# Fourier layer: sequence tables scaled by one root per tile, odd sums as extra columns of the eight-row products, even outputs added by DMA

## The chip, the cores and the metric

One core of a Trainium2 chip runs the whole program. Its engines are PE (matrix products into eight PSUM banks of 128 x 512 f32), DVE and ACT (elementwise work, both can read PSUM), POOL (elementwise work without PSUM, and issuer of the DMA transfers that add to or convert what they write) and SP (issuer of plain DMA transfers). Each engine works its own instructions in order and waits on semaphores for the others. All DMA queues share 16 DMA engines. The metric is the device time of one execution in microseconds (us), the median of several.

## What is computed

Two sequences of 512 tokens and 1024 features each go through two layers. The change lies in the token mixer of the first:

```python
def fourier_mix(h, w_out):
    hg = h.astype(jnp.float32).reshape(B, S, N_FGROUPS, F_GROUP)      # 8 groups of 128 features
    f = jnp.fft.fft2(hg, axes=(1, 3), norm="ortho").real
    return f.reshape(B, S, D_MODEL).astype(h.dtype) @ w_out

x = x + fourier_mix(rms_norm(x, fourier_norm[0]), fourier_w_out[0])
x = x + sq_relu_mlp(rms_norm(x, mlp_norm[0]), mlp_w_up[0], mlp_w_down[0])
x = x + gqa_attention(rms_norm(x, attn_norm[0]), ...)
x = x + sq_relu_mlp(rms_norm(x, mlp_norm[1]), mlp_w_up[1], mlp_w_down[1])
return rms_norm(x, final_norm)
```

## The kernel before

The two sequences q = 0 and q = 1 pass the Fourier layer one after the other, in about the first 90 us; behind that comes the first MLP. All engines' orders in this layer are written out by hand: the code emits instructions in the order in which each engine shall work them.

**Front.** For each sequence the 512 tokens lie in four tiles xa[q, t] of 128 tokens by 1024 features, sorted so that tokens s and S-s meet. Features are sorted so that feature d and its mirror stand in the two halves of 512. `Front(q, c)` handles tiles 2c and 2c+1: `squares` (ACT, sum of squares per token), `gain` (DVE, times the norm's gain), `plus` and `minus` (DVE, sum and difference of the two halves; `plus_there` has a DMA transfer on POOL's queue add one half to the other in place), `chain` (the six small steps of the inverse root), `scale_both` (q = 0, c = 0: ACT multiplies sum, difference and an eight-column extract by the root), and `combine` (DVE, folds the two tiles of c = 1, or of q = 1, into one sum and one difference).

**Sequence transform.** For q = 0 the products are plain f32 (`exact_even`, `exact_odd`): the sums or differences of three folded tiles k against cosine and sine tables, for four blocks j of 128 features, two PSUM banks each. `exact_nyq` does the same for the eight-column extracts, one of the features 64 of each group. For q = 1 the products are split into float32r high and low parts (`seq_part`, `seq_nyq`, `mm3` of three products). ACT and DVE move each block out of PSUM (`seq_evac`).

**Feature transform.** `feat_stage` multiplies each block by the feature tables (even part u, odd part v), adds the eight-row piece (`feat_nyq`) and picks the odd sums (`pickX`, L553) into 72 rows, which `nyq_out` copies into un[q].

**Output products.** `Fold(j)` loads the output weights' two halves, takes the difference on DVE (`minus`) and has a DMA transfer on POOL's queue add the other half in place (L646); high and low parts follow on ACT and DVE. `FoldNyq` prepares 72 rows of weights (wn.w) for un[q], by a trip through HBM (L677, L679). `odd_outs` gives eight odd results, `even_outs` eight even ones, each one PSUM bank. For q = 0 ACT writes the odd results with both signs into xs[0, i] (`odd_put`), DVE adds the even ones to both halves (`even_put`, L726), and then a DMA transfer on POOL's queue adds the input x (`add_input`, L730). For q = 1 the input is loaded into xs[1, i] first (`load_xs`, L168, on SP's queue behind a store of xs[0, 2], L212), and DVE adds even and odd results from PSUM (`even_add`, L708 and L709).

**The norm of the MLP.** During the second transform ACT squares xs[0, i] (`square`, L178), eight times, each time behind an evacuation, and POOL adds the squares (L182). After the third even output of q = 1, PE sums them over partitions (`blocks.root`, L191), DVE and ACT take the root (L141 to L146), and after the fourth PE spreads it by transposes (L199).

Fillers (`idle`, L576) are products whose result nobody reads; 12 run before and 39 after the transposes of the gain (L359).

Of the kernel before, what the change touches and what calls it, by code (L numbers as in the profile page):

```python
# [44 lines left out]
def trunk_kernel(ctx, tc, x_in, xt_in, y_out, tables, rope, gfour, gcol, grow, gfin,  # L45
# [271 lines left out]
    def load_x(q, t, queue=nc.sync):  # L317
        xa[q, t] = slot([P, D], F32)
        queue.dma_start(xa[q, t], x_in[q][t * P : (t + 1) * P, :])
# [22 lines left out]
    def begin():  # L342
# [5 lines left out]
        for t in range(2, 4):  # L348
            load_x(0, t)
        exact_table(5)  # L350
        exact_table(6)
# [39 lines left out]
    def eights(x):  # L391
        return x[:, 0:512:64].unsqueeze(1).broadcast_to([P, 5, 8])

    class Front:


        def __init__(self, q, c):
            self.q, self.c = q, c
            self.ss, self.r = small(2), small(2)
            self.steps = rsqrt_steps(self.r[:, :2], self.ss[:, :2], 2, 1.0 / D)  # L400
            self.xg, self.p, self.m = [None] * 2, [None] * 2, [None] * 2

        def squares(self, i):
            sumsq(xa[self.q, 2 * self.c + i], self.ss[:, i : i + 1])

# [19 lines left out]
        def chain(self, a, b):  # L425
            for step in self.steps[a:b]:
                step()
            if b == 6 and self.c == 0 and self.q:
                self.rm = small(1)
                nc.gpsimd.tensor_mul(self.rm[:, :1], self.r[:, 1:2], mask)  # L430
# [5 lines left out]
        def scale_both(self, i):  # L436
            if i == 0:
                self.n = sm.tile([P, 2, 5, 8], F32, tag="ny", name=nm("ny"), bufs=2, padded_shape=[P, 2, 8, 8])
            for out, x in ((self.p[i], self.p[i]), (self.n[:, i], eights(self.m[i])), (self.m[i], self.m[i])):
                nc.scalar.activation(out, x, AF.Copy, scale=self.r[:, i : i + 1])  # L440
            parts.append((self.p[i], self.m[i], self.n[:, i]))

        def combine(self):
            (p1, p2), (m1, m2), r, w = self.p, self.m, self.r, 8
            stt = nc.vector.scalar_tensor_tensor
            if self.q == 0:
                n = sm.tile([P, 5, 8], F32, tag="ny", name=nm("ny"), bufs=2, padded_shape=[P, 16, 8])
                stt(n, eights(m2), r[:, 1:2], eights(m1), ALU.mult, ALU.add)
# [4 lines left out]
            n = sm.tile([P, 2, 64], F32R, tag="ny", name=nm("ny"), bufs=2)  # L453
            nc.gpsimd.memset(f32(n), 0.0)
# [13 lines left out]
            ny[self.q, self.c] = n  # L468

# [39 lines left out]
    def exact_nyq(k, o):  # L509
        nc.tensor.matmul(o[0:40, :258], parts[k][2].rearrange("p a b -> p (a b)"), cosX[k], start=k == 0, stop=k == 2)  # L510
# [26 lines left out]
    def feat_nyq(u, j, first):  # L537
        nyt = nyqs[0][:, j * P : (j + 1) * P]
        nc.tensor.matmul(u[:, :258], nyt, an, start=first, stop=not first)
        return u  # L540

    def feat_stage(q, j, a, b, an, en, u=None):
        if q == 0:
            nc.tensor.matmul(u[:, :258], ftX[:, :P], a, start=False, stop=True)
        else:
            u = ps()
            mm3(u[:, :258], ft(0)[:, 0:P], ft(1)[:, 0:P], a[:, 0], a[:, 1], True, False)
            feat_nyq(u, j, False)
        v = ps()
        pick = slice(6 - 2 * j, 78 - 2 * j)  # L550
        if q == 0:
            nc.tensor.matmul(v[:, :256], ftX[:, P:], b, start=True, stop=True)
            nc.tensor.matmul(en[0:72, :258], pickX[:, pick], a, start=j == 0, stop=j == 3)  # L553
        else:
            mm3(v[:, :256], ft(0)[:, P:], ft(1)[:, P:], b[:, 0], b[:, 1], True, True)
            ent = tabs[2][:, 516:594][:, pick]
            nc.tensor.matmul(en[0:72, :258], ent, a[:, 0], start=j == 0, stop=False)
            nc.tensor.matmul(en[0:72, :258], ent, a[:, 1], start=False, stop=j == 3)
# [4 lines left out]

    def nyq_out(q, en):
        t = slot([P, 258], F32R)[0:72]
        nc.scalar.copy(t, en[0:72, :258])
        nc.vector.tensor_sub(t[64:72], en[64:72, :258], f32(t[64:72]))
# [3 lines left out]
    nc.gpsimd.memset(f32(an), 0.0)  # L571

    def idle(o, n):

        for _ in range(n):
            nc.tensor.matmul(o[:, :256], filler, filler.unsqueeze(1).broadcast_to([P, 2, P]), start=True, stop=True)  # L576

    def transform(q, mid=lambda: None, hook=lambda at, j: None):
        on, ov = ps(), [(ps(), ps()) for _ in range(3)]
        if q == 0:  # L580
            for k in range(2):
                for j in range(3):
                    exact_even(k, j, ov[j][0])
                exact_nyq(k, on)
                for j in range(3):
                    exact_odd(k, j, ov[j][1])
            mid()
            exact_nyq(2, on)
        else:
            seq_nyq(q, 0, on)  # L590
            for j in range(3):
                seq_part(q, j, 0, *ov[j])
            mid()
            seq_nyq(q, 1, on)
        en = ps()
        nc.scalar.copy(an[0:40], on[0:40, :258])
        nc.vector.tensor_sub(an[32:40], on[32:40, :258], f32(an[32:40]))
        ab = []
        for j in range(3):
            if q == 0:  # L600
                exact_odd(2, j, ov[j][1])
                exact_even(2, j, ov[j][0])
            else:
                seq_part(q, j, 1, *ov[j])
            ab.append(seq_evac(q, *ov[j]))
            hook("seq", j)
        us = [None] * 4
        if q == 0:
            us[0] = feat_nyq(ps(), 0, True)
        feat_stage(q, 0, *ab[0], an, en, us[0])  # L610
        hook("feat", 0)
        o3 = ps(), ps()
        if q == 0:
            for k in range(3):
                exact_even(k, 3, o3[0])
            for k in range(3):
                exact_odd(k, 3, o3[1])
        else:
            for c in range(2):
                seq_part(q, 3, c, *o3)  # L620
        ab.append(seq_evac(q, *o3))
        hook("seq", 3)
        if q == 0:
            us[1:] = [feat_nyq(ps(), j, True) for j in range(1, 4)]
        feat_stage(q, 1, *ab[1], an, en, us[1])
        hook("feat", 1)
        feat_stage(q, 2, *ab[2], an, en, us[2])
        hook("feat", 2)
        feat_stage(q, 3, *ab[3], an, en, us[3])
        nyq_out(q, en)  # L630
        hook("feat", 3)

# [3 lines left out]
    class Fold:  # L636
# [7 lines left out]
        def minus(self):  # L644
            nc.vector.tensor_sub(self.b, self.a, self.b)
            nc.gpsimd.dma_start(self.a, w_four[1, self.j], accum_op=ALU.add)  # L646

        def odd(self):
            hi, lo = lent()
            split(hi, lo, self.b)  # L650
            wo.append((hi, lo))
# [5 lines left out]
        def even_lo(self):  # L657
            w = self.w
            nc.vector.tensor_sub(w[1], self.a, f32(w[0]))
            we[self.j] = w  # L660

    class FoldNyq:
# [7 lines left out]
        def load(self):  # L670
# [7 lines left out]
            for r, i in ((0, 0), (32, 1), (64, 0)):  # L678
# [43 lines left out]

    def even_put(q, fo, o):
# [9 lines left out]
    with tc.manual_schedule(engines={ET.PE, ET.Activation, ET.DVE, ET.Pool, ET.SP}):  # L733
        gr, halves_gr = begin()
        gc = cons.tile([P, 4 * KC], F32, name="gc")
        cosX = [exact[0][:, :258], exact[0][:, 514:772], exact[1][:, 256:514]]
# [1384 lines left out]
```

## Time and profile before

| | |
|---|---|
| median of 3 runs | 1672.95 us (1672.71 to 1673.36) |
| the profiled execution | 1673.12 us, its span 1671.3 us |
| granted PE clock, mean | 0.999 |
| PE busy | 1661.9 us, 99% |
| DVE, ACT, POOL busy | 76%, 52%, 24% |

The page of the profile gives busy shares of the engines over the span, and the chain of work that ended last: from the last instruction back to what released it, and so on. Other views answer for a window of time: each engine's instructions in order of time ("start, duration, engine, line, operation, written <- read, shapes, what ended the idle time before it"), who waited for whom, and the busy time of each engine, the granted clock and the DMA engines' share in given windows. Lines such as L726 are lines of the kernel before. A busy PE is a PE with products in flight; products are pipelined, so the distance between starts says more than the duration of one.

### The profile page before, as it was taken

What the parts mean: (1) busy time and instruction counts of PE and PEld (TensorE: products, weight loads), DVE (VectorE), ACT (ScalarE), POOL (GpSimd) and SP (SyncE); (2) the same over time, 40 slices, a digit from 0 to 9 for tenths busy, and PEclk for the clock granted to TensorE, in tenths of its full rate; (3) what the DMA queues carried; (4) which work ended last, traced back from release to release, by engine and by line L of the source; (5) the groups of instructions that cost most, each with busy time, mean ns of one, the idle gap of its engine ahead of it and who ended that gap; (6) DMA issues with size and microseconds to landing.
All of it is one profiled execution on the core that took longest, in us unless ns stands there. A gap on an engine that the chain in (4) does not pass through costs nothing.

```text
span 1671.3 us, 22288 instructions
## 1 busy us (share of the span) xinstructions
PE 1661.9 (99%) x7843; PEld 1387.8 (83%) x7843; DVE 1267.0 (76%) x1851; ACT 872.1 (52%) x1540; POOL 394.3 (24%) x364
## 2 busy tenths in 40 slices
PE   9999999999999999999999999999999999999998
PEld 8988887888888888888888888888888888888887
DVE  8879776557886869869888877777855487878875
ACT  7766444446342435447688855554454552433334
POOL 3321444221000001325444303004422220000002
PEclk9999999999999999999999999999999999999999
DMA  9843554449775757425501156334544696757532
GB/s 306 257 158 118 204 195 172 151 170 373 250 228 165 248 170 236 168 77 200 166 1 39 64 176 223 117 120 167 211 145 166 221 375 194 233 158 236 178 104 101
DMA packets 122192, 302.48 MB, mean 181 GB/s; under 512 B 12344, under 2 KB 13496, under 8 KB 122080
## 3 DMA queue, kind: packets, MB, share of 16 engines
q1 hardware_dynamic: 98720, 253.53, 43.9%
q0 software_dynamic: 8960, 21.05, 6.0%
q10 hardware_dynamic: 14400, 26.48, 4.2%
q8 instruction: 61, 1.00, 0.2%
q14 instruction: 51, 0.42, 0.1%
HBM read 217.59 MB, written 82.38 MB: 179 GB/s over the span
## 4 chain that ended last, share of the span: by engine, by line
PE 97%; DVE 1%; DMA 0%; ACT 0%; issue 0%; POOL 0%; DVEq 0%; POOLq 0%; ACTq 0%
PE ps L940 74%; PE ps L83 6%; PE ps L81 6%; PE ps L82 6%; PE ps L1535 2%; PE ps L576 0%; PE ps L1514 0%; DMA raw<-w_up 0%; PE ps L191 0%; PE ps L507 0%; PE ps L504 0%; DVE w L87 0%; DVE raw L990 0%; PE ps L199 0%; DVE raw L989 0%
## 5 line engine op out<-in xcount | busy, mean ns | idle before, releaser
L940 PE MATMUL ps<-u,w 128*128 128x512 f32 x4944 | 1130.9, 389 | 1.2 <-DVE t L1018 1.2
L940 PEld LDWEIGHTS ps<-u,w 128*128 128x128 f32 x4944 | 926.6, 188 | 195.9 <-ACT u L973 1.7
L86 ACT CAST w<-raw 128x1024 fp32r<-128x1024 f32 (+1 forms) x216 | 213.7, 994 | 311.5 <-PE ps L940 234.3
L87 DVE TENSOR_TENSOR w<-raw,w 128x1024 fp32r<-128x1024 f32 (+1 forms) x216 | 252.0, 1170 | 75.7 <-ACT w L86 75.4
L86 ACT CAST u<-u 128x1024 fp32r<-128x1024 f32 x144 | 145.0, 1047 | 85.1 <-PE ps L940 36.4
L87 DVE TENSOR_TENSOR u<-u,u 128x1024 fp32r<-128x1024 f32 x144 | 174.3, 1239 | 17.3 <-ACT u L86 16.0
L940 PE MATMUL ps<-u,u 128*128 128x512 f32 x600 | 143.3, 389 | 0.0
L1150 DVE TENSOR_TENSOR u<-ps,u 128x512 f32<-128x512 f32 x160 | 109.9, 688 | 39.8 <-PE ps L940 37.3
L1177 POOL DMA_DIRECT2D raw<-w_sum x32 | 27.7, 865 | 468.2 <-DMA raw<-w_sum 170.8
L1058 POOL TENSOR_TENSOR u<-u 128x512 f32<-128x512 f32 x28 | 37.0, 1321 | 425.9 <-ACT u L955 425.9
L940 PEld LDWEIGHTS ps<-u,u 128*128 128x128 f32 x600 | 112.5, 188 | 24.1 <-ACT u L973 0.4
L81 PE MATMUL ps<-u,u 128*128 128x512 f32 (+2 forms) x340 | 128.7, 380 | 0.0
L83 PE MATMUL ps<-u,u 128*128 128x512 f32 (+2 forms) x340 | 123.7, 365 | 0.0
L82 PE MATMUL ps<-u,u 128*128 128x512 f32 (+2 forms) x340 | 123.6, 365 | 0.0
L182 POOL TENSOR_TENSOR t<-t,t 128x512 f32<-128x512 f32 (+1 forms) x54 | 79.2, 1470 | 187.0 <-ACT t L178 186.1
L954 ACT ACTIVATE t<-t 128x512 f32<-128x512 f32 x64 | 40.5, 632 | 109.2 <-DVE t L1027 95.7
L83 PEld LDWEIGHTS ps<-u,u 128*128 128x128 f32 x340 | 64.2, 189 | 10.5 <-DVE u L87 0.3
L87 DVE TENSOR_TENSOR u<-ps,u 128x512 fp32r<-128x512 f32 (+3 forms) x112 | 68.2, 636 | 5.6 <-ACT u L86 5.0
L82 PEld LDWEIGHTS ps<-u,u 128*128 128x128 f32 x340 | 64.4, 189 | 8.5 <-DVE u L87 0.3
L81 PEld LDWEIGHTS ps<-u,u 128*128 128x128 f32 x340 | 64.4, 189 | 7.8
L1014 DVE TENSOR_TENSOR t<-ps,u 128x512 f32<-128x512 f32 x32 | 22.0, 689 | 59.5 <-PE ps L940 55.8
L86 ACT CAST u<-ps 128x512 fp32r<-128x512 f32 (+3 forms) x112 | 59.5, 557 | 7.7 <-PE ps L1535 6.1
(270 smaller groups left out, 2024.6 us busy)
## 6 DMA issues: line engine op xcount, KB each, us to landing
raw<-w_up SPq DMA_DIRECT2D x80, 512.0 KB, 4.6
u<-spill_t SPq DMA_DIRECT2D x60, 512.0 KB, 6.7
raw<-w_sum SPq DMA_DIRECT2D x56, 512.0 KB, 5.5
u<-spill_b SPq DMA_DIRECT2D x45, 512.0 KB, 6.3
spill_t<-u SPq DMA_DIRECT2D x84, 256.0 KB, 2.0
spill_b<-t ACTq DMA_DIRECT2D x60, 256.0 KB, 4.4
raw<-w_row SPq DMA_DIRECT2D x28, 512.0 KB, 5.0
park<-u SPq DMA_DIRECT2D x24, 512.0 KB, 4.6
```

The lines of the kernel that those rows point to most:

```text
L81: nc.tensor.matmul(out, lh, rh, start=first, stop=False)
L82: nc.tensor.matmul(out, lh, rl, start=False, stop=False)
L83: nc.tensor.matmul(out, ll, rh, start=False, stop=last)
L86: hi = nc.scalar.copy(dst_hi, src)
L87: return hi, eng.tensor_sub(dst_lo, src, f32(dst_hi))
L182: nc.gpsimd.tensor_add(acc[q][:, :n], acc[q][:, :n], s[:, :n])
L940: nc.tensor.matmul(o, w[x][:, sl], h[k][y], start=first and k + i == 0, stop=k == n - 1 and i == 2, skip_group_check=not first)
L954: nc.scalar.activation(t, src, AF.Relu)
L1058: eng.tensor_sub(t[:, 0], b12, b11)
L1150: return nc.vector.tensor_add(x, o, x)
L1177: nc.gpsimd.dma_start(s[:, 1], w[:, 3], accum_op=ALU.add)
L1535: nc.tensor.transpose(pt[:, t * P : (t + 1) * P], probs[t][:, sc * P : (sc + 1) * P], ident)
```

## The change

1. For the first two tiles of q = 0, each has its own root (`root`), and the root is multiplied into the 514 table columns that meet this tile (`table`) and no longer into sum, difference and extract. Tables are laid out anew, so that each tile has its own. The table loads and the tile loads alternate on SP's queue, and the feature table is loaded behind the first weights.
2. The odd sums of the features, which were picked by four products of 72 rows, come as DVE reductions of the sums (`odd_sums`), which ACT writes as 24 more columns per half into the extract (`put_sums`); `exact_nyq` then gives 56 rows, and `put_low` makes un[0] from them. The four products with `pickX` go. The weights' 72 rows move to other places (8, 16, 40).
3. All four blocks of q = 0 run through the sequence transform together in eight PSUM banks (`transform_exact`), and the eight-row products come behind them. The fillers become 23, and 9 more that multiply a zero weight and add to an open bank stand before the third tile.
4. Even results of q = 0 are copied by ACT (`even_put`), and two DMA transfers per pair on POOL's queue add them to xs[0, i] behind the input (`add_even`).
5. Orders change: all four weight differences come together, weights are split later, the gains and sums of q = 1 come earlier on DVE, two of the four tiles of q = 1 are loaded only when the second odd weight is split, the tables of q = 1 are loaded later, and small pieces of work change engines.

```diff
-        for t in range(2, 4):
-            load_x(0, t)
+        load_x(0, 2)
         exact_table(5)
-        exact_table(6)
+        load_x(0, 3)
...
+    def odd_sums(k):
+        s = small(8)
+        x = parts[k][0].rearrange("p (g d i) -> p g d i", g=8, i=2)[:, :, :, 1]
+        nc.vector.tensor_reduce(s, x, AX.X, ALU.add)
+        return s
+
+    def put_sums(k, s):
+        nc.scalar.copy(parts[k][2][:, :, 1:], s.unsqueeze(1).unsqueeze(1).broadcast_to([P, 2, 3, 8]))
...
-    def scale_both(self, i):
+    def table(self, i):
+        t = exact[i][:, :514]
+        nc.scalar.activation(t, t, AF.Copy, scale=self.r[:, i : i + 1])
...
-        nc.tensor.matmul(o[0:40, :258], parts[k][2].rearrange("p a b -> p (a b)"), cosX[k], ...)
+        nc.tensor.matmul(o[0:56, :258], parts[k][2].rearrange("p a b c -> p (a b c)")[:, :56], cosX[k], ...)
...
-            nc.tensor.matmul(en[0:72, :258], pickX[:, pick], a, start=j == 0, stop=j == 3)
...
+    def put_low(on):
+        norm = 1.0 / math.sqrt(S * P)
+        low = un[0]
+        nc.scalar.activation(low[0:56], on[0:56, :258], AF.Copy, scale=norm)
+        nc.vector.scalar_tensor_tensor(low[32:56], on[32:56, :258], norm, f32(low[32:56]), ALU.mult, ALU.subtract)
...
+    def transform_exact(mid, hook):
+        ov = [(ps(), ps()) for _ in range(4)]
+        for k in range(2):
+            for j in range(4):
+                exact_even(k, j, ov[j][0])
+            for j in range(4):
+                exact_odd(k, j, ov[j][1])
+        idle(ov[3][1], 9, an[:, :P])
+        mid()
+        ab = []
+        for j in range(4):
+            exact_odd(2, j, ov[j][1])
+            exact_even(2, j, ov[j][0])
+            ab.append(seq_evac(0, *ov[j]))
+            hook("seq", j)
+        on = ps()
+        for k in range(3):
+            exact_nyq(k, on)
+        put_an(on)
+        put_low(on)
...
     def even_put(q, fo, o):
-        x = xt(q, fo)
-        both = x.rearrange("p (h n) -> p h n", h=2)
-        nc.vector.tensor_add(both[:, :, 1:], o[:, 1:256].unsqueeze(1).broadcast_to([P, 2, 255]), both[:, :, 1:])
-        nc.scalar.copy(x[:, 0:257:256], o[:, 0:257:256])
+        if fo % 2 == 0:
+            even_part[fo // 2] = slot([P, 2, 512], F32)
+        nc.scalar.copy(even_part[fo // 2][:, fo % 2, :257], o[:, :257])
+
+    def add_even(q, i):
+        x, e = xs[q, i], even_part[i]
+        nc.gpsimd.dma_start(x[:, :, :257], e[:, :, :257], accum_op=ALU.add)
+        nc.gpsimd.dma_start(x[:, :, 257:], e[:, :, 1:256], accum_op=ALU.add)
...
-        idle(ps(), 39)
+        idle(ps(), 23)
...
+                fold[1].odd_hi()
+                low = fold[1].odd_lo()
+                for t in range(2, NT):
+                    behind(load_x(1, t), low, sync=True)
...
-        for fo in range(4, 6):
-            odd_put(0, fo, o[fo])
-        g0.combine()
         for k in range(4):
             table(k)
...
-        even(5)
-        g1.scale(slice(1, 2))
-        even(6)
         g1.combine()
         g1.split_hi()
+        even(5)
+        add_even(0, 2)
+        g1.split_lo()
+        even(6)
         even(7)
-        g1.split_lo()
+        add_even(0, 3)
```

POOL's queue, before, from the tables of the second sequence to the first addition of squares. u_579 and u_612 are sums of tiles of q = 1 (`plus_there`), u_441 to u_444 are xs[0, 0] to xs[0, 3] with their input:

```order
L329 DMA u_594<-dcos 128x774
L329 DMA u_596<-dsin 128x1024
L329 DMA u_598<-dalt 128x594
L329 DMA u_600<-dfeat 128x512
L419 DMA u_579<-u_579 128x512
L419 DMA u_612<-u_612 128x512
L730 DMA u_441<-xt 128x1024
L730 DMA u_442<-xt 128x1024
L730 DMA u_443<-xt 128x1024
L454 MEMSET ny_748 128x128
L730 DMA u_444<-xt 128x1024
L182 TENSOR_TENSOR t_846<-t_846,t_862 128x512
```

The same stretch now, from the end of the first tile's odd outputs to the last tile sum (L438 is `plus_there`, L784 `add_input`; u_441, u_443, u_445 and u_447 are now xs[0, 0] to xs[0, 3]):

```order
L438 DMA u_554<-u_554 128x512
L784 DMA u_441<-xt 128x1024
L438 DMA u_582<-u_582 128x512
L784 DMA u_443<-xt 128x1024
L438 DMA u_596<-u_596 128x512
L329 DMA u_601<-dcos 128x774
L329 DMA u_603<-dsin 128x1024
L329 DMA u_605<-dalt 128x594
L329 DMA u_607<-dfeat 128x512
L438 DMA u_616<-u_616 128x512
L784 DMA u_445<-xt 128x1024
L784 DMA u_447<-xt 128x1024
```

And right behind it, the additions of the even outputs (L780 and L781, `add_even`) up to the first addition of squares:

```order
L780 DMA u_441<-u_639 128x2x257
L781 DMA u_441<-u_639 128x2x255
L780 DMA u_443<-u_670 128x2x257
L781 DMA u_443<-u_670 128x2x255
L780 DMA u_445<-u_728 128x2x257
L781 DMA u_445<-u_728 128x2x255
L780 DMA u_447<-u_773 128x2x257
L781 DMA u_447<-u_773 128x2x255
L182 TENSOR_TENSOR t_859<-t_859,t_875 128x512
```

The first two input additions moved ahead of the tables, the tables moved behind three tile sums, and eight transfers now stand between the last input addition and the additions of squares.

ACT's order in the second transform, before: a square of xs[0, 0] stands between two evacuations (L86), and waits for one transfer of POOL's queue (DMASW is such a transfer's semaphore).

```order
L86 CAST u_840<-ps_797 128x258 [waits PE_49]
L86 CAST t_841<-ps_798 128x256 [waits PE_49]
L178 ACTIVATE t_846<-u_441 128x512 [waits DMASW0_49]
L86 CAST u_856<-ps_799 128x258 [waits PE_49]
L86 CAST t_857<-ps_800 128x256 [waits PE_49]
```

Now:

```order
L86 CAST u_853<-ps_810 128x258 [waits PE_49]
L86 CAST t_854<-ps_811 128x256 [waits PE_49]
L178 ACTIVATE t_859<-u_441 128x512 [waits DMASW4_49,DMASW5_49,DMASW1_49,Pool_49]
L86 CAST u_869<-ps_812 128x258 [waits PE_49]
L86 CAST t_870<-ps_813 128x256 [waits PE_49]
```

No row moved; the square now waits for three transfers, the input's and the two of the even outputs.

SP's store of xs[0, 2] and what stands behind it, before and then now:

```order
L212 DMA park<-u_443 128x1024 [waits DMAHW6_49,DMASW2_49,Activation_49]
L168 DMA u_780<-xt 128x1024 [waits DMAHW7_49,DMAHW1_49]
L168 DMA u_782<-xt 128x1024 [waits DMAHW2_49,DMAHW0_49]
L168 DMA u_784<-xt 128x1024 [waits DMASW7_49]
L168 DMA u_786<-xt 128x1024 [waits DMASW1_49]
```

```order
L212 DMA park<-u_445 128x1024 [waits DMASW1_49,DMASW2_49,DMASW0_49,DMAHW6_49,Activation_49,Pool_49]
L168 DMA u_793<-xt 128x1024 [waits DMAHW7_49,DVE_49]
L168 DMA u_795<-xt 128x1024 [waits DMAHW5_49,DMAHW0_49,Activation_49]
L168 DMA u_797<-xt 128x1024 [waits DMAHW1_49,PE_49]
L168 DMA u_799<-xt 128x1024 [waits DMAHW2_49,PE_49]
```

The order is the same; the store's wait now takes in the transfers that add the even outputs to xs[0, 2].

More of the change, by code (lines that the diff above doesn't have):

```diff
@@ L751, in trunk_kernel @@
+        f0.gain(0, 1, halves_gr[1])
+        nc.scalar.copy(gr[:, 512:], halves_gr[1])
+        f0.root(0, 2, 6)
+        f0.table(0)
+        f0.plus(0)
+        f0.minus(0)
+        f0.squares(1)
+        wn.load()
+        fold = [Fold(0)]
+        exact_table(6)
+        fold += [Fold(j) for j in range(1, 4)]
+        for t in range(2):
+            load_x(1, t)
+        nc.sync.dma_start(gc, gcol)
+        f0.gain(1)
+        f0.root(1, 0, 3)
         f1.squares(0)
-        f0.scale_both(0)
@@ L753, in trunk_kernel @@
[L753 removed]
+        f0.plus(1)
+        f0.root(1, 3, 4)
         f0.minus(1)
[L755 to L756 removed]
+        f0.root(1, 4, 6)
+        f0.table(1)
         f1.squares(1)
         f1.chain(1, 2)
[L759 removed]
+        f0.low(0)
+        f0.low(1)
+        ftX = exact[2][:, :256]
+        f1.gain(0)
         f1.minus(0)
         f1.gain(1)
[L762 removed]
+        sums3 = []
         def mid():
             f1.chain(0, 1)
+            f1.chain(2, 3)
```

330 lines of the change are left out of this document (167 added, 163 removed).

## The prediction

> **What bounds the kernel now.** I read the busy shares and the chain that ended last first, then the waits of PE in the first 230 us (the change ends before 100 us; behind that each engine runs the same instructions in the same order as before).
>
> ```profile
> PE 1661.9 (99%) x7843; PEld 1387.8 (83%) x7843; DVE 1267.0 (76%) x1851; ACT 872.1 (52%) x1540; POOL 394.3 (24%) x364
> ...
> PE 97%; DVE 1%; DMA 0%; ACT 0%; issue 0%; POOL 0%; DVEq 0%; POOLq 0%; ACTq 0%
> ```
>
> ```profile
> PE ps L576 <- DVE mask L369: 1.2, 1, 1.2
> PE ps L199 <- DVE s L146: 0.2, 1, 0.2
> ```
>
> PE is the chain: it stands still for 1.4 us in 230, and once it has started it runs without a hole until the root of the second sequence. So a change in the Fourier layer can gain only PE work that it takes away, and loses whatever hole it makes. The second thing to read is the DMA engines, by stage (columns behind the engines: granted PE clock, DMA share, GB/s):
>
> ```profile
> 41.00:53.40 12.40, 12.40 (x105) 12.40 (x105) 11.87 (x25) 9.51 (x30) 3.87 (x5) 1.00 0.64 163
> 53.40:65.30 11.90, 11.90 (x102) 11.88 (x101) 9.24 (x23) 9.84 (x28) 6.93 (x7) 1.00 1.01 215
> 65.30:72.60 7.30, 7.30 (x63) 7.30 (x62) 4.03 (x13) 6.48 (x15) 4.08 (x4) 1.00 0.98 367
> ```
>
> From 53.4 us on they are full, at 215 GB/s while POOL's adding transfers run and at 367 while plain loads run. Only between 45 and 51 us are they empty, as half-microsecond windows show (window, its length, clock, DMA share, GB/s):
>
> ```profile
> 42.00:42.50 0.50, 1.00 1.22 441
> 45.50:46.00 0.50, 1.00 0.00 0
> ...
> 46.50:47.00 0.50, 1.00 0.49 86
> 47.00:47.50 0.50, 1.00 1.04 184
> 47.50:48.00 0.50, 1.00 1.09 193
> 48.00:48.50 0.50, 1.00 0.39 62
> 48.50:49.00 0.50, 1.00 0.00 0
> ...
> 50.00:50.50 0.50, 1.00 0.00 0
> 57.00:57.50 0.50, 1.00 0.98 197
> ```
>
> The four windows from 46.5 us are one transfer alone: a 256 KB piece added in place within the on-chip memory (L419). It occupies all 16 engines for half of 0.49+1.04+1.09+0.39, 1.5 us, or 1.4 us at its steady 188 GB/s; I use 1.4. A 512 KB addition of the input at the 197 GB/s of the last row takes 2.6 us. Such a transfer thus costs twice what a plain load of its size does (441 GB/s above).
>
> **What the change takes from PE.** The chain of waits gives the prices:
>
> ```profile
> 1.17 2.93 PE ps L576 x12
> 5.81 5.40 PE ps L576 x39
> 12.52 0.56 PE ps L510 x2
> 22.28 0.43 PE ps L553 x2
> 30.77 0.12 PE ps L82
> 70.21 0.79 PE ps L191 x8
> 72.66 0.44 PE ps L199 x4
> ```
>
> Sixteen of the 39 fillers go: 16 x 5.40/39 = 2.2 us. The four picking products go (L553, each a pair of records, 0.43): 1.7 us. Nine fillers at 0.12 to 0.14 come in: 1.2 us. The products of eight-row sums grow from 40 rows to 56, which changes no column count, so I leave 0.56 each. Sum: 2.7 us less work, the most that this change can gain, and 0.16% of the time. Part of it goes to waiting. The third pair of products needs the combined tile:
>
> ```profile
> 17.20 0.75 DVE L449 SCALAR_TENSOR_TENSOR t<-t,s,t 128x512 f32<-128x512 f32 x1
> ```
>
> DVE reaches that row through the same gains, sums and differences as before, with one more chain of five small operations (0.16 us each), and without a hole before or now; so the tile is ready at about 17.8 to 18 us again, while PE with fillers is there at 17.3. I take 0.5 us for this, and the first product of the odd outputs comes 2.2 us earlier than now. Scaling a table (ACT, 514 columns) instead of two sums (512 each) is one ACT operation less per tile, and the tables are scaled before PE arrives; no cost. The three new reductions (128x8 from 256 each) have no row; between the smallest and the largest DVE operation they cost 0.2 to 1.2 us, and I take 0.4 by their element count. They stand behind the combination, where the eight products of the third pair (eight times 0.43, 3.5 us) hide them; without this cover up to 1.2 us would show.
>
> Taking the even outputs off DVE frees eight additions (5.2 us with the copies) at a place where DVE is full, but PE did not wait for DVE there, so it is worth nothing on PE's path.
>
> **What the change adds to the DMA engines.** Each pair of even outputs is now copied by ACT and added by two transfers on POOL's queue, 257 and 255 columns of two rows: eight transfers of 262 KB, the size and kind of the L419 piece. At 1.4 us they are 11.2 us of full DMA. Their rows are 1 KB where L419's are 2 KB, which no row here prices. Bounds: 0.65 us each if they moved at the plain 441 GB/s, 2.8 if a 1 KB row cost as much as a 2 KB one; I take 1.4, the nearest row.
>
> [...]
>
> What stands around them:
>
> ```profile
> 34.54 0.86 POOL L419 DMA_DIRECT2D u<-u  x1 [1.73 <-DVE t L423]
> 49.78 0.89 POOL L419 DMA_DIRECT2D u<-u  x1 [3.54 <-PE ps L697]
> 50.42 2.04 POOL L730 DMA_DIRECT2D u<-xt  x2
> 57.59 0.88 POOL L730 DMA_DIRECT2D u<-xt  x1 [3.03 <-ACT u L596]
> 59.72 4.04 POOL L182 TENSOR_TENSOR t<-t,t 128x512 f32<-128x512 f32 x3 [1.25 <-ACT t L178]
> 64.20 5.42 POOL L182 TENSOR_TENSOR t<-t,t 128x512 f32<-128x512 f32 x4 [0.44 <-ACT t L178]
> ```
>
> ```profile
> 62.62 0.33 SPq L212 DMA_DIRECT2D park<-u  x1
> 63.05 2.23 SPq L168 DMA_DIRECT2D u<-xt  x4
> ```
>
> ```profile
> 68.83 0.43 DVE L708 TENSOR_TENSOR u<-ps,u 128x257 f32<-128x257 f32 x1 [2.20 <-DMA u<-xt]
> ...
> 71.04 0.16 DVE L141 TENSOR_SCALAR s<-ps 128x4 f32<-128x4 f32 x1
> ...
> 72.14 0.16 DVE L146 SCALAR_TENSOR_TENSOR s<-ps,s 128x4 f32<-128x4 f32 x1
> ```
>
> The first of the L419 kind still goes out at about 35.1 us (34.54 above; its root's first step now stands ahead of it), since ACT's squares and the gain in front of it stay where they were. From there the queue must carry four of them (5.6 us), four inputs (10.4), the four tables (2,904 columns of 512 B, 1.49 MB, at 441 GB/s 3.4): 19.4 us, as before. Now add 11.2. Two holes remain, since the first input waits for ACT's odd outputs (about 1 us) and the second L419 kind for DVE's four low parts of the weights (1.3). With 1.3 us from issue to motion the queue is empty at 35.1 + 1.3 + 19.4 + 11.2 + 2.3 = 69.3 us; before, it was so at about 63.5.
>
> SP's queue is in order: its store of xs[0,2] waits for the sixth of the eight additions, and the loads of the second sequence's input stand behind that store. The sixth lands 2.8 us before the end, with 0.4 us of receipt at 66.9, where the row above has 62.62: 4.3 us later. Two additions still share the engines with the load, about 1 us. So the input lands 5.3 us later, at about 74.1; DVE's first addition, which already waits 2.20 us for it, starts then, and three additions and the root behind it lead to PE's L199 3.8 us later, with 0.2 us of slack. PE's 2.2 us in hand do not help, since PE waits at L199.
>
> The same backlog holds ACT: its square of the first pair now waits for the first two additions (35.1 + 1.3 + 2.3 + 19.4 + 2.8 + 0.4 = 61.3 us against 57.93), and the evacuation behind it holds PE's accumulation banks:
>
> ```profile
> 57.93 0.64 ACT L178 ACTIVATE t<-u 128x512 f32<-128x512 f32 x1
> 58.47 0.36 ACT L86 CAST u<-ps 128x258 fp32r<-128x258 f32 x1
> ```
>
> That makes PE wait some 3 us at its fourth block of sequence products (3.4 us late and 2.2 early, less some 2.5 that its eight banks hold), and POOL's additions of squares, which start when its last issue is out, end about 4 us later than 69.6. These two alone would cost 3 to 4 us; they run beside the 5.3 and do not add to it.
>
> **Sum.** The profiled execution took 1673.12 us (span 1671.3, 1.8 around it), so one like it would take 1673.12 + 5.3 = 1678.4; the median of the runs shown, 1672.95, lies 0.17 below that execution, so I predict **1678.3 us**. Ten pieces stand ahead of the store, so 0.1 us more or less for each moves it by 1.0, and the two holes are mine to within 1: own range 1676.5 to 1681.
>
> **Rivals.** (1) The additions are cheap, and the gain shows. Place: the square of the first pair and SP's store. It decides itself at whether the sixth addition lands before about 61 us. The empty 45 to 51 us speak for it, and the plain rate of 441 GB/s; against it, the tables and the last L419 kind now go out in that very gap. Then the 2.2 us stay: 1670.8. (2) The additions run at the plain rate but start behind the inputs all the same: the first square at 60 us, 2 us late, the store at about 63; PE loses 1 to 3 us there: 1673 to 1676, no difference. (3) A 1 KB row costs as much as a 2 KB one: 22.4 us instead of 11.2, less the two behind the store: 8.4 us more than forecast, 1687. [...] (4) The PE clock falls in the new hole. The first twelve fillers took 0.244 us each and the warm ones 0.12; the first 6 us of PE's work ran at half speed, about 3 us lost. If the hole of 3 us starts such a phase anew: 1681.3. [...]
>
> **How the numbers follow.** Forecast 0.48, (1) 0.13, (2) 0.20, (3) 0.10, (4) 0.09. A difference of 0.2%, 3.3 us, is about what can be told from none. Faster by that would need more than the 2.7 us of work removed: 0.04. Within it are (1) but for that, (2), and the low edge of the forecast: 0.33. Slower: 0.63. The range 1670.5 to 1685 leaves out (3) and the edges.
>
> **What would show it.** Right: ACT's first square of the Fourier outputs waits on a DMA until about 61 us; SP's store starts near 67 instead of 62.6; DVE's first even addition of the second sequence near 74; holes of PE at its fourth sequence block and at the spreading transposes; the odd products some 2 us earlier than the row here:
>
> ```profile
> 29.24 0.47 PE L81 MATMUL ps<-u,u 128*128 128x256 f32 x1
> ```
>
> Wrong, if those squares don't wait, if the DMA share between 45 and 60 us stays below one, or if the odd products start no earlier, since then the front is the bound.

## The result, and the profile after

| | before | changed |
|---|---|---|
| median (6 runs each) | 1672.51 us | 1711.87 us |
| lowest to highest | 1671.79 to 1673.36 | 1710.33 to 1713.33 |
| the profiled execution, its span | 1673.12, 1671.3 | 1710.33, 1708.6 |
| granted PE clock, mean | 0.999 | 0.987 |

The changed kernel is slower by the ratio 1.0235 (in brackets, here and below, the 95% interval: [1.0222, 1.0248]), 39.4 us, seven times the forecast loss of 5.3. The busy times and the shares of the chain that ended last, from its page:

```profile
PE 1671.5 (98%) x7828; PEld 1395.6 (82%) x7828; DVE 1261.5 (74%) x1851; ACT 872.3 (51%) x1542; POOL 401.4 (23%) x376
...
PE 93%; issue 2%; DVE 2%; ACT 1%; DMA 1%; POOL 1%; DVEq 0%; POOLq 0%; ACTq 0%
```

"Issue" has 2% of the chain where it had 0%: an engine that waits for nothing that the profile shows. POOL's instructions in order of time show where (start, duration, line; in brackets the idle time before and what ended it):

```profile
59.65 1.22 POOL L780 DMA_DIRECT2D u<-u  x1 [4.84 <-issue]
63.92 1.22 POOL L781 DMA_DIRECT2D u<-u  x1 [3.06 <-issue]
68.08 1.20 POOL L780 DMA_DIRECT2D u<-u  x1 [2.94 <-issue]
...
84.50 1.20 POOL L780 DMA_DIRECT2D u<-u  x1 [2.92 <-issue]
94.14 1.21 POOL L781 DMA_DIRECT2D u<-u  x1 [8.43 <-issue]
94.89 7.16 POOL L182 TENSOR_TENSOR t<-t,t 128x512 f32<-128x512 f32 x5
```

The additions of the even parts go out one every 4.1 to 4.3 us, the last 9.6 us behind the seventh; before, two inputs went out 1 us apart (the x2 row of L730 in the prediction). The DMA engines are not what holds them. Half-microsecond windows around the first addition (window, its length, busy times of PE, PEld, DVE, ACT and POOL, then clock, DMA share, GB/s):

```profile
61.00:61.50 0.50, 0.50 (x4) 0.50 (x4) 0.33 (x1) 0.14 (x1) 0.00 (x0) 0.50 0.15 25
61.50:62.00 0.50, 0.50 (x4) 0.50 (x4) 0.09 (x1) 0.15 (x1) 0.00 (x0) 0.50 1.16 169
62.00:62.50 0.50, 0.50 (x5) 0.50 (x4) 0.24 (x1) 0.24 (x2) 0.00 (x0) 0.50 1.25 177
62.50:63.00 0.50, 0.50 (x4) 0.50 (x4) 0.29 (x2) 0.36 (x1) 0.00 (x0) 0.50 1.10 158
63.00:63.50 0.50, 0.50 (x6) 0.50 (x6) 0.32 (x1) 0.00 (x0) 0.00 (x0) 0.92 0.07 6
63.50:64.00 0.50, 0.50 (x7) 0.50 (x6) 0.00 (x0) 0.00 (x0) 0.08 (x1) 1.00 0.00 0
```

It moves for half of 0.15+1.16+1.25+1.10+0.07, 1.9 us, and the engines then stand empty until the next is issued at 63.92, when the first has landed (3.9 us median from issue to landing). SP's queue, in order, and ACT's squares hang on it:

```profile
84.39 0.33 SPq L212 DMA_DIRECT2D park<-u  x1
84.81 2.24 SPq L168 DMA_DIRECT2D u<-xt  x4
```

```profile
67.85 0.63 ACT L178 ACTIVATE t<-u 128x512 f32<-128x512 f32 x1 [4.99 <-DMA u<-u]
...
76.07 0.63 ACT L178 ACTIVATE t<-u 128x512 f32<-128x512 f32 x1 [5.99 <-DMA u<-u]
...
84.37 0.63 ACT L178 ACTIVATE t<-u 128x512 f32<-128x512 f32 x1 [5.52 <-DMA u<-u]
...
96.68 0.63 ACT L178 ACTIVATE t<-u 128x512 f32<-128x512 f32 x1 [11.15 <-POOL t L182]
```

The store (L212) starts at 84.39 where it started at 62.62, and at that moment SP's loads start too and share the engines with the last two additions. The last square of the four is held another way: POOL works in order, so its sums (L182) stand behind the issue of the eighth addition at 94.14, and this square waits 11.15 us for them. PE waits behind ACT, as its waits say (who waited for whom: us in total, times, longest; the 11.0 is for an evacuation behind that last square), and by stage (window, length, PE busy, clock, DMA share, GB/s):

```profile
PE ps L81 <- ACT u L86: 14.4, 2, 11.0
PE ps L81 <- DVE u L87: 6.7, 2, 3.6
PE ps L81 <- ACT u L776: 3.7, 1, 3.7
PE ps L191 <- POOL t L182: 1.9, 1, 1.9
```

```profile
54.00:58.00 4.00, 0.30 (x3) 0.78 1.06 178
58.00:68.00 10.00, 8.13 (x47) 0.75 0.63 104
68.00:85.00 17.00, 9.32 (x44) 0.66 0.43 62
85.00:104.00 19.00, 7.42 (x30) 0.50 1.01 332
```

PE's spreading transposes (L199) start at 110.50 instead of 72.50, 38 us late, and from there on the kernels run alike. The DMA share from 58 to 85 us is below two thirds: no backlog, but round trips.

### The profile page after: what moved, and what is told of

It is laid out like the page before. It is cut to its first block, busy times and chain, and to the rows that moved or that the text cites. A ratio compares the mean times of both kernels' runs of the same rounds, so it can differ in the third digit from the quotient of the medians.

```text
span 1708.6 us, 22284 instructions
## 1 busy us (share of the span) xinstructions
PE 1671.5 (98%) x7828; PEld 1395.6 (82%) x7828; DVE 1261.5 (74%) x1851; ACT 872.3 (51%) x1542; POOL 401.4 (23%) x376
## 3 DMA queue, kind: packets, MB, share of 16 engines
q1 hardware_dynamic: 98720, 253.53, 42.9%
## 4 chain that ended last, share of the span: by engine, by line
PE 93%; issue 2%; DVE 2%; ACT 1%; DMA 1%; POOL 1%; DVEq 0%; POOLq 0%; ACTq 0%
PE ps L1023 74%; PE ps L81 5%; PE ps L83 5%; PE ps L82 5%; PE ps L1618 2%; DMA u<-u 1%; PE ps L1597 0%; PE ps L191 0%; POOL u L780 0%; DVE u L429 0%; ACT w L702 0%; ACT t L130 0%; PE ps L604 0%; ACT u L690 0%; PE ps L199 0%
## 5 line engine op out<-in xcount | busy, mean ns | idle before, releaser
L86 ACT CAST w<-raw 128x1024 fp32r<-128x1024 f32 (+1 forms) x216 | 213.6, 994 | 307.8 <-PE ps L1023 244.4
L86 ACT CAST u<-u 128x1024 fp32r<-128x1024 f32 (+1 forms) x140 | 140.8, 1046 | 85.4 <-PE ps L1023 33.8
L87 DVE TENSOR_TENSOR u<-u,u 128x1024 fp32r<-128x1024 f32 (+1 forms) x140 | 169.3, 1239 | 17.4 <-ACT u L86 16.9
L81 PE MATMUL ps<-u,u 128*128 128x512 f32 (+2 forms) x340 | 130.2, 385 | 7.2 <-ACT u L776 3.7
L1023 PEld LDWEIGHTS ps<-u,u 128*128 128x128 f32 x600 | 112.5, 188 | 24.0 <-ACT u L1056 0.4
L83 PE MATMUL ps<-u,u 128*128 128x512 f32 (+2 forms) x340 | 124.9, 368 | 0.0
L82 PE MATMUL ps<-u,u 128*128 128x512 f32 (+2 forms) x340 | 124.9, 368 | 0.0
L182 POOL TENSOR_TENSOR t<-t,t 128x512 f32<-128x512 f32 (+1 forms) x54 | 79.5, 1477 | 188.3 <-ACT t L178 187.3
L81 PEld LDWEIGHTS ps<-u,u 128*128 128x128 f32 x340 | 65.7, 193 | 15.6 <-ACT u L776 3.9
L178 ACT ACTIVATE t<-u 128x512 f32<-128x512 f32 (+1 forms) x64 | 37.9, 602 | 77.7 <-DMA u<-u 21.5
L83 PEld LDWEIGHTS ps<-u,u 128*128 128x128 f32 x340 | 65.4, 192 | 10.5 <-DVE u L87 0.2
L82 PEld LDWEIGHTS ps<-u,u 128*128 128x128 f32 x340 | 65.7, 193 | 8.5 <-DVE u L87 0.2
```

What stands on the lines that cost most here:

```text
L81: nc.tensor.matmul(out, lh, rh, start=first, stop=False)
L82: nc.tensor.matmul(out, lh, rl, start=False, stop=False)
L83: nc.tensor.matmul(out, ll, rh, start=False, stop=last)
L86: hi = nc.scalar.copy(dst_hi, src)
L87: return hi, eng.tensor_sub(dst_lo, src, f32(dst_hi))
L178: made = nc.scalar.activation(s[:, :n], xt(q, fo)[:, :n], AF.Square)
```

## The experiments

The profile counts 272 packets for one such addition, of two rows per partition, and 144 for one of L419, with one row: one for each row and 16 small ones (under 512 B). My theory after this reading, called "room" below: POOL's queue has a bounded room for the rows of its transfers (a descriptor each, by the theory), so two of these additions do not fit together, and each is issued only when the one before has landed. I took a number of the build, 1024 here, for the size of this room. The runs show what changing it does; what it counts they do not show. The medians of before were 1672.3 to 1672.6 us beside every run.

**More room.** One number of the build, in two sizes (1152 is shown; 1088 is the same edit, run when 1152 had given 1690.53 us):

```diff
-    nc = _bacc.Bacc("TRN2", ..., num_devices=1, dynamic_dma_scratch_size=1024)
+    nc = _bacc.Bacc("TRN2", ..., num_devices=1, dynamic_dma_scratch_size=1152)
```

> [...] Theory (room): in the changed kernel one addition with two rows per partition leaves too little of that room for a second, so each is issued only when the one before has landed, one every 4.1 us. An eighth more room lets a second stand beside it: the eight additions go out within 15 to 20 us instead of 34.5 (59.65 to 94.14), SP's store starts near 73 instead of 84.39, time 1680 to 1690. Rival (rate): the 1 KB rows themselves are slow or the engines are full; the room changes nothing, 1712. Rival (program waits: each addition waits on a semaphore for the one before): 1712 too.

> [...] Theory (room): what counts is whether two additions of two rows per partition fit together. If they need little more than 1024, this is as fast as 1152: 1689 to 1692. If they need between 1088 and 1152 it is as slow as the changed kernel: 1710 to 1714. A time in between would speak against a step, and for something that grows with the room.

Measured: 1690.53 us with 1152 (ratio 1.0107 [1.0092, 1.0122]) and 1693.24 with 1088 (1.0123 [1.0108, 1.0139]). POOL with 1152:

```profile
61.95 1.21 POOL L781 DMA_DIRECT2D u<-u  x1 [3.74 <-issue]
63.35 1.22 POOL L780 DMA_DIRECT2D u<-u  x1 [0.19 <-issue]
65.93 1.20 POOL L781 DMA_DIRECT2D u<-u  x1 [1.37 <-issue]
67.53 1.19 POOL L780 DMA_DIRECT2D u<-u  x1 [0.40 <-ACT t L178]
```

Nothing but this number differs, and the additions now go out in pairs, two per 4 us. 21.3 us come back, and the time lies half a microsecond above my band. So a limit that this number sets was the cause of the waits; the two rivals had 1712. It is mostly a step between 1024 and 1088: by the medians the first 64 are worth 18.6 us and the further 64 only 2.7, with intervals that overlap. 1088 lies 1 us above the band I gave for it.

**One row per partition.** Same eight additions, rows of 2 KB; and sixteen additions of one 1 KB row:

```diff
         nc.scalar.copy(even_part[fo // 2][:, fo % 2, :257], o[:, :257])
+        nc.scalar.copy(even_part[fo // 2][:, fo % 2, 257:], o[:, 1:256])
...
-        nc.gpsimd.dma_start(x[:, :, :257], e[:, :, :257], accum_op=ALU.add)
-        nc.gpsimd.dma_start(x[:, :, 257:], e[:, :, 1:256], accum_op=ALU.add)
+        for k in range(2):
+            nc.gpsimd.dma_start(x[:, k], e[:, k], accum_op=ALU.add)
```

> The changed kernel, but ACT writes the even part out in full (257 columns, then the 255 mirrored ones) and the eight additions are of 512 columns each: the same eight, the same bytes (256 KB), one row of 2 KB per partition instead of two of about 1 KB. Theory (room): 128 rows are half as many descriptors, two or three additions fit at once, and they go at about 1.5 us each: SP's store near 71, time 1677 to 1685. Rival (rate by row length): better as well, about the same. Rival (program waits): one every 4.1 us still, 1712.

```diff
+        for k in range(2):
+            nc.gpsimd.dma_start(x[:, k, :257], e[:, k, :257], accum_op=ALU.add)
+            nc.gpsimd.dma_start(x[:, k, 257:], e[:, k, 1:256], accum_op=ALU.add)
```

> The changed kernel, but each of the eight additions is cut in two: sixteen additions of one row of about 1 KB per partition (128 KB each). Theory (room): 128 rows each, three fit at once, so they are held up by POOL's issue alone (0.9 to 1.2 us each): sixteen in 15 to 20 us, SP's store near 73 to 77, time 1680 to 1690. Rival (rate: 1 KB rows are slow): not faster than the changed kernel, 1710 or more. Rival (program waits, one round trip of some 3.5 us for each): 56 us, 1725 or more.

Measured: 1683.67 us (1.0066 [1.0049, 1.0082]) and 1689.90 (1.0102 [1.0087, 1.0117]). POOL with 2 KB rows, then with sixteen 1 KB rows:

```profile
66.87 0.85 POOL L782 DMA_DIRECT2D u<-u  x1 [0.40 <-ACT t L86]
68.15 0.85 POOL L782 DMA_DIRECT2D u<-u  x1 [0.43 <-ACT u L86]
69.60 0.87 POOL L782 DMA_DIRECT2D u<-u  x1 [0.60 <-ACT u L86]
```

```profile
66.95 0.85 POOL L781 DMA_DIRECT2D u<-u  x1
68.05 0.87 POOL L782 DMA_DIRECT2D u<-u  x1 [0.24 <-issue]
```

Twice as many transfers with the same short rows are 22 us faster than the changed kernel: neither row length nor a wait of each for the one before explains its 4.1 us. In the stretch shown the 2 KB pieces leave 1.3 to 1.45 us apart, the 1.4 us of the prediction; before it the gaps are 1.2 to 3.7 us, and all eight go out within 13.8 us.

**The additions alone**, put into the kernel before:

```diff
+            nc.gpsimd.memset(xs[0, i][:, :, 0:257:256], 0.0)
...
                 add_input(0, fo // 2)
+                add_even(0, fo // 2)
```

> The kernel before with one part of the change alone: ACT copies the even parts, and behind each input two additions of two rows per partition (257 and 255 columns) add them on POOL's queue. All else as before. Theory (room): eight pieces that go out one by one, with inputs between them that must also wait; from 51 us on 8 x 4.1 us and some more: 25 to 40 us above before, 1698 to 1712. Rival (the loss needs the new order too): at most the 11 us of added traffic that the prediction priced, 1678 to 1684.

Measured: 1717.07 us (1.0266 [1.0251, 1.0281]), above my band. This one part alone costs 44.5 us, more than the whole change. It is worse than in the changed kernel, where all four inputs had gone out before the first addition: here POOL sits idle for 5.9 to 6.8 us between an input and the first addition to the same tile, and for 2.9 more before the second (8.46 before the last of the eight). Whether the first of these waits is for room or for the input itself to land, this run does not separate:

```profile
62.65 1.43 POOL L736 DMA_DIRECT2D u<-xt  x1
69.99 1.22 POOL L732 DMA_DIRECT2D u<-u  x1 [5.91 <-issue]
74.10 1.21 POOL L733 DMA_DIRECT2D u<-u  x1 [2.89 <-issue]
```

**The last two additions.** SP's first store waits for the eighth addition instead of the sixth:

```diff
-        put_away(0, 2)
+        put_away(0, 3)
...
-                if fo != 2:
+                if fo != 3:
```

> The changed kernel with SP's first store exchanged: the store that opens SP's queue is that of the fourth pair instead of the third, so the reload of the second sequence's input and the weight loads cannot start before the last addition has landed. Theory (contention at the end): the seventh and eighth addition took 9.3 and 8.9 us because these loads share the engines with them; without them they take 4.1 each, the last lands near 93 instead of 103, and the sums start 8 to 10 us earlier, though the reload now starts at 93 and binds instead: 1702 to 1708. Rival (the last two are slow for another reason): no gain or a loss, 1711 to 1722.

Measured: 1702.96 us (1.0183 [1.0169, 1.0197]). The seventh and eighth go out like the others, and the store follows at 93.16:

```profile
85.13 1.20 POOL L780 DMA_DIRECT2D u<-u  x1 [2.93 <-issue]
89.24 1.21 POOL L781 DMA_DIRECT2D u<-u  x1 [2.91 <-issue]
```

So 8.9 us of the loss, net of what the later store costs, hang on SP's loads beside the last two additions: loads that come earlier made the kernel later.

**The even outputs back on DVE**, all the rest of the change kept (of the input's additions, which move behind the even outputs, only the new place is shown):

```diff
-        nc.scalar.copy(even_part[fo // 2][:, fo % 2, :257], o[:, :257])
+        nc.vector.tensor_add(both[:, :, 1:], o[:, 1:256].unsqueeze(1).broadcast_to([P, 2, 255]), both[:, :, 1:])
+        nc.scalar.copy(x[:, 0:257:256], o[:, 0:257:256])
...
             even_put(0, fo, even_outs(0, [fo])[0])
+            if fo % 2:
+                add_input(0, fo // 2)
...
-            add_even(0, i)
```

> The changed kernel with the even outputs put back as before: DVE adds them from PSUM, ACT copies columns 0 and 256, and each input is added when its pair of even outputs is done. All the rest of the change stays (tables scaled by a root per tile, odd sums, 72-row products, queue order). Theory: the whole loss hangs on the additions, and the rest is worth the 2 us that the odd products start earlier, if nothing behind takes it: 1670.5 to 1673. Rival: other parts of the change (the later second fold of the input, the new order of ACT) lose time by themselves: 1675 or more.

Measured: 1677.81 us (1.0030 [1.0019, 1.0042]). My theory fell here, the rival held: something else loses time. PE waits 4.4 us for ACT's two-column copies of even outputs (L777 there). The changed kernel has this hole as well, 3.7 us at 54.3 to 58.0, ahead of the first addition; its links, from POOL, DVE, ACT and PE:

```profile
50.88 0.88 POOL L438 DMA_DIRECT2D u<-u  x1 [0.78 <-PE ps L83]
...
55.61 0.75 DVE L485 SCALAR_TENSOR_TENSOR u<-u,s,u 128x512 f32<-128x512 f32 x1 [4.86 <-DMA u<-u]
...
56.40 0.62 ACT L499 CAST u<-u 128x512 fp32r<-128x512 f32 x1 [4.72 <-DVE u L485]
...
57.58 0.92 ACT L776 COPY u<-ps 128x257 f32<-128x257 f32 x3
...
58.00 0.58 PE L81 MATMUL ps<-u,u 128*128 128x258 f32 x1 [3.70 <-ACT u L776]
```

Read from below: PE waits for a bank that ACT's copies (L776) must free, they stand in ACT's order behind the split (L499) of a tile that DVE folds (L485) from the fourth in-place addition (L438), which lands late.

**The tables out of that addition's way**, once with the even outputs on DVE and once with the 2 KB additions:

```diff
+        for k in range(4):
+            table(k)
         g0.gain(1)
         g0.scale(slice(0, 1))
...
-        for k in range(4):
-            table(k)
```

> The changed kernel with the even outputs back on DVE (1677.8), and the four transform tables issued before the second fold of the sequence's input instead of after the third. Theory: what is left of the loss there is PE's hole of 4.4 us, which comes since the fourth fold (in place, 256 KB) lands only at 54.6 us behind the tables, with 1.7 us more for the half clock behind the hole. With the tables in the empty 38 to 43 us the fourth fold lands near 52.5, the hole goes, and the 2 us gained at the front show: 1670 to 1672.5. Rival: the hole comes from the order of ACT and DVE themselves (even outputs behind the combination): 1676 to 1678.

> The changed kernel with additions of one 2 KB row per partition (1683.7) and the four tables issued before the second fold. Theory: the first hole of PE there (4.0 us, behind ACT's copy of an even output that waits for the fourth fold) goes, and its half clock with it; the rest, the queue of eight additions at 1.3 to 1.4 us each in front of SP's store, stays: 1676 to 1680, near the 1678.3 that was predicted for the changed kernel. Rival: the additions set the end alone and the hole is hidden beside them: 1682 to 1684.

Measured: 1676.85 us (1.0026 [1.0015, 1.0036]) with the even outputs on DVE and 1682.57 (1.0061 [1.0046, 1.0076]) with 2 KB additions: the rivals' numbers, both times. With the even outputs on DVE, the fourth in-place addition went out at 46.26 instead of 47.85 and DVE no longer waits for it, but holes stay: the late addition alone does not make them. PE's waits and its stages (columns as above) in this version are:

```profile
PE ps L81 <- ACT u L777: 3.2, 3, 1.7
```

```profile
54.00:56.00 2.00, 0.34 (x3) 1.00 0.93 131
56.00:58.00 2.00, 0.83 (x5) 0.69 0.91 160
58.00:60.00 2.00, 2.00 (x11) 0.50 0.92 143
60.00:62.00 2.00, 2.00 (x11) 0.50 1.06 188
62.00:64.00 2.00, 2.00 (x13) 0.61 1.01 234
```

Three holes, none over 1.7 us, and behind the last, from about 57.6 to 63.4 us, work at clock 0.50, with products 0.215 us apart that were 0.12 apart before the holes: another 2.6 us, an estimate by these distances. With 3.2 us of holes, less the 2.1 gained at the front, that is 3.7, where the medians differ by 4.3.

**The front alone.** The new front, and from the odd outputs on the order of before:

```diff
         g0.chain(0, 1)
-        g0.gain(0)
-        g0.chain(2, 3)
-        g0.minus(0)
-        g0.plus_there(0)
...
+        for i in range(2):
+            g0.gain(i)
+            g0.minus(i)
+            g0.plus_there(i)
+        fold[0].even_hi()
+        fold[1].even_hi()
+        g0.chain(2, 6)
...
+        g1.chain(2, 6)
+        even(4)
+        g1.scale(slice(0, 1))
+        even(5)
+        g1.scale(slice(1, 2))
+        even(6)
+        g1.combine()
```

> The front of the change alone: tables scaled by a root per tile, odd sums in 72-row products, fillers, the weights' folds behind the exact products; behind the odd products the order and the kind of work is that of the kernel before (even outputs on DVE, the second sequence's fold in two steps right behind one another, tables and inputs at their old places in POOL's queue). Theory: PE starts the odd products 2.1 us earlier, and the hole of 3 to 4 us at the even outputs, which came from their new order on ACT and DVE, is gone: 1670.5 to 1672.5 (less than 2.1 gained, since the reload of the second sequence's input, which waits for the third input addition, then binds). Rival: DVE, which now makes the folds of the weights later, is late for the second sequence's folds, and a hole stays: 1674 to 1678.

Measured: 1673.25 us, ratio 1.0003 [0.9994, 1.0012]: no difference, and between the bands of theory and rival. The holes between 53 and 58 us are gone, so the order behind the odd outputs made them; which of its moves did, this run does not separate. Where the 2 us of the front went is seen in PE's two waits at the first even outputs, in its start of the sums over partitions (L191; below it that of the kernel before), and in DVE's first even addition of the second sequence:

```profile
39.95 0.39 PE L81 MATMUL ps<-u,w 128*128 128x258 f32 x1 [0.67 <-ACT u L769]
42.45 0.39 PE L83 MATMUL ps<-u,w 128*128 128x258 f32 x1 [0.51 <-DVE w L705]
70.41 0.95 PE L191 MATMUL ps<-ones,t 128*128 128x2 f32 x8
```

```profile
70.05 0.95 PE L191 MATMUL ps<-ones,t 128*128 128x2 f32 x8
```

```profile
69.81 0.43 DVE L756 TENSOR_TENSOR u<-ps,u 128x257 f32<-128x257 f32 x1 [2.80 <-DMA u<-xt]
```

PE has 339 products from the first odd product to L191 in both kernels. They take 40.81 us before (29.24 to 70.05) and 43.11 here (27.30 to 70.41). By the distances between starts 2.2 us of that are lost at the first even outputs, from 39.0 to 42.9, where PE waits for ACT's copies of the odd outputs (L769) and for DVE's low parts of the weights (L705). So the 2 us are gone by 43 us. The reloaded input binds as well, but later: L756 starts at 69.81, where it started at 68.83 in the kernel before.

**The reload earlier**, to beat both kernels: SP's first store that of the second or of the first pair (the second is shown, as an edit of the front alone).

```diff
-        put_away(0, 2)
+        put_away(0, 1)
...
-                if fo != 2:
+                if fo != 1:
```

> The front of the change alone (1673.25), with SP's first store that of the second pair instead of the third. Theory: the 2.1 us of the front are lost only at DVE's first even addition of the second sequence, which waits 2.80 us for the reloaded input; the reload stands behind SP's store, and that behind the third input addition. The second addition lands some 2.5 us earlier, so the reload goes out near 60.5 instead of 63.1, shares the engines with the last two additions, and lands 1 to 2 us earlier: 1671 to 1672.5. Rival (the engines are the bound, the loads only push the additions back): 1673 to 1675.

> The same with the store of the first pair ahead: the reload can start near 58. Theory: input there in time, 1670.5 to 1672. Rival: the loads and three of the additions share full engines, the last additions land later and hold ACT's squares: 1673 to 1677.

Measured: 1672.78 us (0.9999 [0.9990, 1.0008]) and 1675.01 (1.0015 [1.0006, 1.0024]). With the second pair the store starts at 60.84, and the wait for the input shrinks to 1.07 us, but PE reaches L191 only at 70.75, so there is nothing to win: the time lies between the two bands, no different from the kernel before. With the first pair the kernel is slower, as the rival said: ACT's last two squares wait 1.31 us for an addition of the input, and L191 waits 0.51 us for POOL's sums. No version here beats the kernel before.

## Why the prediction was wrong

- **The failing step** is "Now add 11.2" in the part on the DMA engines: eight pieces at 1.4 us, carried back to back. The price of a piece was the smaller miss (1.9 us of full DMA in the changed kernel instead of 1.4; 1.3 to 1.45 us apart with one row of 2 KB). What failed is that they did not follow one another: they took 34.5 us from the first issue to the eighth and 43.4 to the last landing, since with the build's number at 1024 each waited for the one before (one every 4.1 us; two per 4.0 to 4.3 at 1088 and 1152), and SP's loads slowed the last two (9.3 and 8.9 us to land, 3.8 to 3.9 for the others). I had taken from the transfers of before that POOL issues without waiting for a landing; all of those have one row per partition, and these have two. I asked what a short row costs in time, never whether two rows per partition let fewer transfers go out at a time.
- **The store on SP's queue**: right in kind (it waits for the sixth addition, the reload stands behind it), 84.39 instead of the predicted 66.9. **ACT's first square**: 67.85 instead of 61.3. The prediction had the backlog hold PE beside the reload, at no cost of its own; in fact the squares' waits carried the end, by way of POOL's sums (L191 waits for L182), which stand behind the eighth issue. A slip besides: the lower bound of a piece, 0.65 us, should read 0.59 (262 KB at 441 GB/s); the forecast does not use it.
- **The new order behind the odd outputs** has no term in the sum, so it was put at nothing without a reason. It made holes that PE did not have: with the even outputs on DVE, PE takes 47.63 us from the first odd product to L191 (27.24 to 74.87), where the kernel before takes 40.81. Putting the old order back is worth 4.6 us (1677.81 against 1673.25). That the even outputs taken off DVE are by themselves "worth nothing on PE's path" no run tests.
- **The front**: right in the sum, by luck in its parts. The first odd product starts at 27.12 us instead of 29.24, 2.1 us earlier where 2.2 was forecast. But the transform's first product starts 3.0 us earlier (8.09 instead of 11.05), where sixteen fillers were priced at 2.2, and from there to the odd products PE needs 0.8 us more, where the terms added up to nothing; the wait for the combined tile was 1.0 us instead of 0.5. Whether "PE's 2.2 us in hand do not help" no run shows: with the front alone they are gone at 43 us, before the reload counts.

```profile
27.12 0.34 PE L81 MATMUL ps<-u,u 128*128 128x256 f32 x1
```

- **Rivals.** (1) and (2), cheap additions, fell. (3), a 1 KB row at the price of a 2 KB one, fell in its mechanism: the pieces moved at 158 to 177 GB/s, where the 2 KB rows of before had 184 and 193, a tenth slower and not half; summed over its windows a piece holds the engines 1.9 us, that of before 1.5, a quarter more. (4), the clock, came true; its cost here is not separated, but PE waits for data through much of its slow time (from 85 to 104 us it is busy for 7.42 us at clock 0.50). In the version with the even outputs on DVE and the tables moved it cost 2.6 us, by the estimate above.

The ladder of medians divides the 39 us: 28 go with one row per partition (1711.87 to 1683.67), 6 more with the even outputs back on DVE (1677.81), 4.6 with the old order behind the odd outputs (1673.25).

## What to carry to other kernels

Before moving work to POOL's DMA queue, count rows per partition, not only bytes: here an addition of two rows cost a whole round trip, 4.1 us, where its data moved for 1.9, and one of the same size in one row went out 1.3 to 1.45 us behind the one before (in the stretch shown). A gap that the profile calls "issue" in front of DMA instructions (2.9 us and more), with idle DMA engines beside it, was the sign here. And when a piece of work changes engines, read again who stands behind whom in the new engine's order: here holes of PE came from a new order alone, and putting the old one back was worth 4.6 us. And before a late wait is blamed for a gain that does not show, compare when PE gets there: with the front alone the gain was lost 27 us earlier.

## What the hardware showed that was not expected

- Two rows per partition: with the build's number at 1024 one such addition was in flight at a time (one every 4.1 us, 3.8 to 3.9 from issue to landing before SP's loads started); with 1088 and 1152 two went out per 4.0 to 4.3 us.
- Two additions of 256 KB that shared the engines with plain loads of 512 KB took 9.3 and 8.9 us to land; with the loads held back (SP's first store that of the fourth pair) each went out 4.1 to 4.2 us behind the one before, and the store that waits for the eighth started 3.9 us behind that one's issue (89.24 and 93.16).
- With the even outputs on DVE and the tables moved, the granted clock stood at 0.50 for some 6.8 us (its fall lies inside the last hole) behind three holes of 0.37, 1.66 and 1.17 us within 4.4 us, none of them long; with the front alone, two holes of 0.67 and 0.51 us, 2.5 us apart, left it at 1.00.
